# Group norm of the RWKV heads along the free dimension, in an fp32 decoder step on one Trainium2 core

## The chip, the cores and the metric

The kernel runs on one core of one Trainium2 chip. A time is the device time of one execution in microseconds (us); where several executions were timed, the median is given with the lowest and the highest. Names of engines are those of the profile: PE is TensorE's matmul stream and PEld its weight loads, DVE is VectorE, ACT is ScalarE, POOL is GpSimd, SP is SyncE, which here only issues DMAs. PEclk is the TensorE clock that was granted, as a share of full speed.

## The reference, cut to what matters

One trunk layer of a hybrid decoder on 256 prompt tokens and 8 single decode tokens, all in fp32: a half-step SwiGLU, a mixing stage in which attention heads and RWKV-7 heads read one projection and are joined by one output projection, and a second half-step SwiGLU. The change lies in the RWKV heads (16 heads of 64 columns, worked on as 8 pairs):

```python
def wkv_scan(S0, r, logw, k, v, kk, a):
    def step(S, inp):
        r_t, lw_t, k_t, v_t, kk_t, a_t = inp
        sa = jnp.einsum('bhij,bhj->bhi', S, -kk_t)
        S = (S * jnp.exp(lw_t)[:, :, None, :] + sa[..., None] * (kk_t * a_t)[:, :, None, :]
             + v_t[..., None] * k_t[:, :, None, :])
        return S, jnp.einsum('bhij,bhj->bhi', S, r_t)
...
    S, y = wkv_scan(wkv0, r, logw, k, v, kk, a)
    mean = jnp.mean(y, axis=-1, keepdims=True)
    var = jnp.mean((y - mean) ** 2, axis=-1, keepdims=True)
    yn = ((y - mean) * lax.rsqrt(var + GN_EPS)).reshape(B, T, RWKV_WIDTH) * ln_w.astype(f32) + ln_b.astype(f32)
    bonus = jnp.sum(r * k * r_k.astype(f32), axis=-1, keepdims=True) * v
    out = (yn + bonus.reshape(B, T, RWKV_WIDTH)) * g
```

The mean and the variance of the group norm are taken over the 64 columns of one head, for each token apart.

## The kernel before, in words

Every large product is a `gemm` (L141): weights come in chunks of four 128x128 blocks. For a chunk, SP starts a 256 KB load into `raw` (six deep), ACT casts it to `hi` (L137), DVE subtracts to `lo` (L64; four deep), and PE does three matmuls of 128x264 per block into a PSUM tile `acc` (three deep): twice with `hi`, once with `lo`. Line L80 is the helper that issues every matmul, L64 that of two-operand DVE and POOL operations, L67 that of `scalar_tensor_tensor`, L74 that of ACT's functions, so groups in the profile are told apart by the names of their tiles.

The stages follow each other: first SwiGLU, mixing, output projection, second SwiGLU. Mixing (`mixing_body`, L362) runs 38 tiles of the input projection in the order of `SEQ`; after each chunk `tick()` advances every spawned task by one step, and a task is a Python generator that gives up its turn at each `yield`. `pause(n)` gives up n turns. So the constants at the top of the file (`LAG`, `P1`, `P2`, `DWAIT`, `PW`, `HOP`, `NSTEP`) say how many chunks of the gemm lie between two steps of a task. The gemm's matmuls are what stands between the tasks' small products on PE; the order in which the instructions of each engine finally stand is made by the framework's scheduler, and each engine then works its instructions in that order.

The tasks that matter here work on four batches of two head pairs:

- `prep` (L445), one per pair: keys, decays and the tables for the scan; among its small products are `m<-PT,...` to `XD` and `uv`.
- `chain` (L570), one per batch: a triangular inverse on DVE (tiles `X`, `Xt`, `st`; one `yield` per `NSTEP` steps), then 32x32 products (`m<-PT,gm`, `m<-TT,W`), 64x64 products into `ub`, `wb`, `pb`, `gb`, `pN` and `pY`, and a loop over three token blocks in which the state `S` is carried and `pY` is added to. `pY` is the recurrence's output, one 128x512 PSUM tile for a batch. Before, its columns are tokens and its partitions the 64 columns of a head.
- `gnorm` (L727), one per pair, in batches 0, 1 and 2 with `small`: `y` (128x264, the 8 decode columns included) is copied out of `pY` (L694), a product with `cm` from the constants `C` subtracts the mean (`m<-y,C`), ACT squares, three narrow products sum the squares (`m<-C,t`, in `sums`), ACT takes the root, DVE the reciprocal of 88x6, and `spread` (L433) writes that to DRAM (`dr<-s`) and reads it back copied to all 64 partitions of each head (`t<-dr`); then DVE multiplies (`y<-y,t`) and two more DVE operations apply the weights, the bonus and the gate. In batch 3 a product with `bo` sums and spreads the squares in one, and the reciprocal is one of 128x264.
- `turned`, `kvtask`, `attend`, `dec_scores`, `dec_attend`: the attention heads and the decode tokens.

PSUM tiles named `m` form a ring of five banks that all small products share. The output projection takes the eight attention tiles between the pairs 0 to 3 and the pairs 4 to 7 (`PASS`), so batches 2 and 3 are due last.

Of the kernel before, what the change touches and what calls it, by code (L numbers as in the profile page):

```python
# [24 lines left out]
HALF = (slice(0, 64), slice(64, 128))  # L25
# [22 lines left out]
VMU, VKK, VKA, VA0, VRK, VLW, VLB, VSK, VSD = 64, 90, 98, 106, 114, 122, 130, 138, 154  # L48
# [4 lines left out]
def body(tc, I, O):  # L53
    nc = tc.nc
    V, A, G, TE, SP = nc.vector, nc.scalar, nc.gpsimd, nc.tensor, nc.sync
# [3 lines left out]
    def uid(s):  # L59
        cnt[0] += 1  # L60
        return f"{s}{cnt[0]}"

    def tt(e, out, a, b, op):
        return e.tensor_tensor(out=out, in0=a, in1=b, op=op)  # L64

    def stt(out, a, s, b, op0, op1):
        return V.scalar_tensor_tensor(out=out, in0=a, scalar=s, in1=b, op0=op0, op1=op1)  # L67
# [5 lines left out]
    def act(out, in_, f, **k):  # L73
        return A.activation(out=out, in_=in_, func=f, **k)  # L74

    def bc(ap, shape):
        return ap.broadcast_to(list(shape))

    def mm(out, lhsT, rhs, start=True, stop=True, **k):
        return TE.matmul(out, lhsT, rhs, start=start, stop=stop, **k)  # L80
# [20 lines left out]
    def pause(n):  # L101
        for _ in range(n):
            yield

    with ExitStack() as ctx:
# [4 lines left out]
        dp = ctx.enter_context(tc.tile_pool(name="dp", bufs=1, space=bass.MemoryType.DRAM))  # L110
# [16 lines left out]
        def mp():  # L127
            return pp.tile([P, 512], F32, tag="m", bufs=NM, name=uid("m"))
# [33 lines left out]
        eps = cp.tile([P, 2], F32, name="eps")  # L162
# [8 lines left out]
        def vc(i):  # L171
            return vec[:, i:i + 1]
# [189 lines left out]
        def mixing_body(mx, n2, n3, XD, XR):  # L362
# [3 lines left out]
            def ring(shape, tag, bufs):  # L366
                return mx.tile(list(shape), F32, tag=tag, bufs=bufs, name=uid(tag))
# [6 lines left out]
            ident, bo, cm = C[:, CID:CID + P], C[:, CBO:CBO + P], C[:, CCM:CCM + P]  # L374
# [26 lines left out]
            mixed = [None] * 16  # L401
# [21 lines left out]
            la, sgl = fix((P, T), "la"), fix((P, T), "sgl")  # L423
# [1 line left out]
            class Batch:  # L425
                pass

            def sums(sq):
                sm = mp()
                for j in range(3):  # L430
                    mm(sm[0:88, j * 2:j * 2 + 2], sq[:, j:T:3], bo[:, 0:P:64])
                return sm[0:88, 0:6].rearrange("p (j h) -> p h j", h=2)

            def spread(s, to):
                d = dp.tile([2, T], F32, tag=uid("dr"), name=uid("dr"))
                SP.dma_start(d.rearrange("h (p j) -> p h j", j=3), s)
                yield from pause(HOP[0])
                for h in range(2):
                    behind(SP.dma_start(to[HALF[h]], bc(d[h:h + 1], (64, T))))
                yield from pause(HOP[1])  # L440

            def c4(x):
                return x[:, :NP].rearrange("p (c t) -> p c t", c=4)

            def prep(p, bt, k, xrr, xk, xv):  # L445
# [9 lines left out]
                kk, b = tmp(), tmp()  # L455
# [6 lines left out]
                W, Wi = tmp((P, 4, 65)), tmp((P, 4, 64))  # L462
# [40 lines left out]
                tt(V, bv, bps[:, :T], xv, ALU.mult)  # L503
                A.copy(rk[:, T:], bps[:, T:T + 2 * NB])
# [37 lines left out]
                yield  # L542
                gv, dps = mp(), mp()
                for i in range(NB):
                    c, g = i // 2, i % 2
# [24 lines left out]
            def chain(bt):  # L570
# [47 lines left out]
                yield  # L618
                ps = mp()
                for j in range(4 * n):  # L620
                    for h in range(2):
# [5 lines left out]
                yield from pause(P1)  # L627
                Ys = [yb[bt.p0 + k] for k in range(n)]
                uv = bt.UV
                N = ring((P, n, 4, 64), "N", 1)  # L630
                ub, wb = mp(), mp()
# [9 lines left out]
                A.copy(W, v[:, :, 1:4, :])  # L641
# [33 lines left out]
                yield  # L675
                S = N[:, :, 0, :]
                for c in range(1, 4):
                    ps = mp()
                    for k in range(n):
                        x = (k * 4 + c) * 64  # L680
                        for h in range(2):
                            r, o = HALF[h], HALF[1 - h]
                            mm(ps[r, k * 64:k * 64 + 64], PT[r, k, c - 1, :], S[r, k])
                            mm(pY[o, x:x + 64], S[r, k], bt.KR[k][r, 1, c, :], False, True, skip_group_check=True)
                    Z, Sn = ring((P, n, 64), "Z", 2), ring((P, n, 64), "S", 3)
                    for k in range(n):
                        stt(Z[:, k], S[:, k], wc[:, bt.p0 + k, c:c + 1], N[:, k, c, :], ALU.mult, ALU.add)
# [3 lines left out]
                    yield  # L691
                for k in range(n):
                    for h in range(2):
                        (A.copy, V.tensor_copy)[h](Ys[k][HALF[h], :NP], pY[HALF[1 - h], k * NP:(k + 1) * NP])  # L694
# [4 lines left out]
                gps = []  # L699
                gs = [gnorm(Ys[k], SMALL[bt.i]) for k in range(n)]  # L700
                for _ in range(PW[3] + 1 + SMALL[bt.i] * sum(HOP)):
                    for g in gs:
                        next(g)
                    yield
                for k in range(n):
                    p, o = bt.p0 + k, Ys[k]
                    gp = mp()
                    mm(gp[:, :T], g2s[k], sgl)
                    stt(o, o, vc(VLW + p), bt.bv[k], ALU.mult, ALU.add)
                    stt(o, o, vc(VLB + p), gp[:, :T], ALU.add, ALU.mult)  # L710
                    mixed[p] = o
                if len(bts) == nbat and bt is bts[-1]:
                    spawn(turned())
                yield
# [9 lines left out]
                    A.copy(XR[HALF[h], 4], xt[0:64, HALF[h]])  # L724
                yield

            def gnorm(y, small):  # L727
                yp = mp()
                mm(yp[:, :T], cm, y)
                r = tmp()  # L730
                act(r, yp[:, :T], AF.Square)
                if small:
                    A.copy(y, yp[:, :T])
                    yield from pause(PW[3])
                    s = ring((88, 2, 3), "s", 4)
                    act(s, sums(r), AF.Sqrt, scale=1.0 / 64, bias=eps[0:88, 1:2])
                    V.reciprocal(s, s)
                    yield from spread(s, r)
                    tt(V, y, y, r, ALU.mult)
                    yield  # L740
                    return
                yield from pause(PW[3])
                vp = mp()
                mm(vp[:, :T], bo, r)
                act(r, vp[:, :T], AF.Sqrt, scale=1.0 / 64, bias=eps[:, 1:2])
                V.reciprocal(r, r)
                tt(V, y, yp[:, :T], r, ALU.mult)
                yield

            kT, Vt = [None] * 2, [None] * 2  # L750
            dkv = fix((P, 2, 2, NB), "dkv")
# [394 lines left out]
```

## Time and profile before

| | |
|---|---|
| median of 3 executions (lowest, highest) | 1952.91 us (1950.18, 1953.28) |
| profiled execution, its own time | 1950.27 us |
| its span, first to last instruction | 1948.5 us |
| PE busy | 1934.1 us (99%) |
| DVE, ACT, POOL busy | 1307.8, 1035.9, 260.6 us |
| mean granted TensorE clock | 0.997 |

The profile is of one execution. Its waits list how long an engine stood idle and which event ended that; its chain follows the last instruction back, at each step to what released it; its windows give the busy time of every engine in a stretch of the span, with the granted clock. An fp32 matmul leaves more than one record, so a count in the chain (x2) is of records and not of products.

### The profile page before, as it was taken

The page shows a single profiled execution, that of the slowest core. Times are in us where ns is not written, and L with a number is a line of the kernel's source. Part 1 is how long each engine was busy: PE and PEld are TensorE (multiplying, and loading weights), DVE is VectorE, ACT ScalarE, POOL GpSimd, SP SyncE. Part 2 cuts the span into 40 slices and gives each one's busy share as a digit, 9 for nine tenths or more (in the row PEclk, how much of TensorE's full clock was granted, in tenths as well). Part 3 has the DMA queues.
Part 4 walks back from the last instruction along what each step waited for, and adds up shares of the span by engine and source line. Part 5 has one row for each costly group of instructions (what it writes and reads, how often), then busy time and mean ns, then how long its engine had stood idle before and what let it go on. Part 6 is the DMA issues. An engine that isn't in the chain of part 4 may idle for free.

```text
span 1948.5 us, 45522 instructions
## 1 busy us (share of the span) xinstructions
PE 1934.1 (99%) x17131; PEld 1917.4 (98%) x17131; DVE 1307.8 (67%) x2591; ACT 1035.9 (53%) x2069; POOL 260.6 (13%) x382
## 2 busy tenths in 40 slices
PE   9999999999999999999999999999999999999998
PEld 9999999999999999999899999999999999999998
DVE  5865555655556567799867877866666666666665
ACT  5644444444444456666477645644444444444445
POOL 0401102010010112231102100210101001010012
PEclk9999999999999999999999999999999999999999
DMA  7666666665656567565545656566666666666664
GB/s 240 179 194 193 186 194 195 185 189 179 188 182 184 184 193 233 162 173 155 146 133 151 200 157 183 176 187 188 192 191 193 187 193 190 193 194 184 195 181 149
DMA packets 220958, 358.10 MB, mean 184 GB/s; under 512 B 34866, under 2 KB 74434, under 8 KB 220738
## 3 DMA queue, kind: packets, MB, share of 16 engines
q1 hardware_dynamic: 214226, 346.59, 59.6%
q10 hardware_dynamic: 6512, 8.61, 1.3%
q8 instruction: 134, 2.20, 0.4%
q14 instruction: 86, 0.70, 0.1%
HBM read 347.48 MB, written 9.70 MB: 183 GB/s over the span
## 4 chain that ended last, share of the span: by engine, by line
PE 98%; DMA 1%; DVE 1%; ACT 0%; issue 0%; SPq 0%; DVEq 0%; ACTq 0%
PE acc L80 89%; PE m L80 8%; DMA x<-in_x 0%; DMA t<-dr 0%; DVE y L64 0%; DMA ld<-in_cv 0%; PE m L535 0%; DVE lo L64 0%; SPq L581 0%; DMA ld<-in_bias 0%; ACT t L74 0%; PE m L493 0%; PE m L528 0%; PE m L812 0%; ACT hi L137 0%
## 5 line engine op out<-in xcount | busy, mean ns | idle before, releaser
L64 DVE TENSOR_TENSOR lo<-raw,hi 128x512 fp32r<-128x512 f32 (+1 forms) x1288 | 875.6, 683 | 522.8 <-ACT hi L137 499.4
L137 ACT CAST hi<-raw 128x512 fp32r<-128x512 f32 (+1 forms) x1288 | 776.8, 606 | 803.3 <-PE acc L80 724.5
L80 PE MATMUL acc<-x,hi 128*128 128x264 f32 x4840 | 900.2, 287 | 1.5 <-DVE st L64 1.3
L80 PEld LDWEIGHTS acc<-x,hi 128*128 128x128 f32 x4840 | 753.3, 189 | 5.0 <-ACT t L74 1.5
L80 PE MATMUL acc<-x,lo 128*128 128x264 f32 x2420 | 692.8, 286 | 0.0
L80 PE MATMUL acc<-h,hi 128*128 128x264 f32 x2752 | 495.0, 284 | 0.0
L80 PEld LDWEIGHTS acc<-x,lo 128*128 128x128 f32 x2420 | 458.3, 189 | 1.5 <-DVE lo L64 0.4
L80 PEld LDWEIGHTS acc<-h,hi 128*128 128x128 f32 x2752 | 424.4, 189 | 0.0
L80 PE MATMUL acc<-h,lo 128*128 128x264 f32 x1376 | 387.8, 284 | 0.0
L80 PEld LDWEIGHTS acc<-h,lo 128*128 128x128 f32 x1376 | 259.2, 189 | 0.0
L64 POOL TENSOR_TENSOR t<-t,t 128x264 f32<-128x264 f32 x74 | 79.8, 1078 | 1095.6 <-DVE t L64 958.2
L80 PE MATMUL acc<-y,hi 128*128 128x264 f32 x648 | 122.7, 284 | 0.0
L80 PE MATMUL acc<-o,hi 128*128 128x264 f32 x648 | 120.1, 284 | 0.0
L80 PE MATMUL acc<-kv,hi 128*128 128x264 f32 x582 | 109.7, 284 | 0.0
L80 PEld LDWEIGHTS acc<-y,hi 128*128 128x128 f32 x648 | 101.2, 189 | 0.1
L80 PEld LDWEIGHTS acc<-o,hi 128*128 128x128 f32 x648 | 100.1, 189 | 0.0
L67 DVE SCALAR_TENSOR_TENSOR x<-acc,x 128x264 f32<-128x264 f32 x192 | 81.2, 427 | 24.5 <-PE acc L80 23.6
L80 PE MATMUL acc<-y,lo 128*128 128x264 f32 x324 | 92.0, 284 | 0.0
L80 PE MATMUL acc<-o,lo 128*128 128x264 f32 x324 | 92.0, 284 | 0.0
L80 PEld LDWEIGHTS acc<-kv,hi 128*128 128x128 f32 x582 | 90.2, 189 | 0.1
L64 DVE TENSOR_TENSOR t<-acc,t 128x264 f32<-128x264 f32 x156 | 67.4, 432 | 32.8 <-PE acc L80 32.7
L80 PE MATMUL acc<-kv,lo 128*128 128x264 f32 x291 | 82.9, 285 | 0.0
(300 smaller groups left out, 1637.5 us busy)
## 6 DMA issues: line engine op xcount, KB each, us to landing
raw<-in_gu SPq DMA_DIRECT2D x688, 256.0 KB, 3.3
raw<-in_dn SPq DMA_DIRECT2D x224, 256.0 KB, 2.9
raw<-in_win SPq DMA_DIRECT2D x152, 256.0 KB, 3.5
raw<-in_dn SPq DMA_DIRECT2D x160, 192.0 KB, 2.8
raw<-in_wout SPq DMA_DIRECT2D x64, 256.0 KB, 3.5
xsp<-x ACTq DMA_DIRECT2D x16, 132.0 KB, 3.7
x<-xsp SPq DMA_DIRECT2D x16, 132.0 KB, 4.0
ld<-in_sT SPq DMA_DIRECT2D x16, 128.0 KB, 4.4
```

The lines of the kernel that those rows point to most:

```text
L64: return e.tensor_tensor(out=out, in0=a, in1=b, op=op)
L67: return V.scalar_tensor_tensor(out=out, in0=a, scalar=s, in1=b, op0=op0, op1=op1)
L80: return TE.matmul(out, lhsT, rhs, start=start, stop=stop, **k)
L137: A.copy(hi[:, :w], raw[:, :w])
```

## The change

Only the RWKV tasks change.

1. The operands of the products into `pY` are swapped, so that tokens lie on partitions and a head's 64 columns along the free dimension.
2. `gnorm` is now one task per batch, the same for all four: DVE sums `pY` over the free dimension (TENSOR_REDUCE, 128x512 to 128x8), subtracts the mean into the tile `N`, ACT squares, DVE sums the squares, ACT takes the root, DVE the reciprocal (128x24, decode columns included) and multiplies `N`. Sixteen 64x64 products with an identity turn a batch back into a PSUM tile `tp`. The 8 decode columns of each pair still go through `cm` and `bo`, 16 columns for a batch.
3. `sums`, `spread` and their hop through DRAM are gone: six `dr<-s` and twelve `t<-dr` transfers.
4. The copy of `W` moves from ACT to DVE, and the two copies of `uv` swap engines.
5. Pauses: `NSTEP` falls from 5 to 3 (a turn is given up ten times in the inverse, before six times), new pauses `PZ` and `PX` stand where one `yield` stood, and others change their length.

```diff
-LAG = (11, 7, 7, 7)
-P1 = 1
-P2 = 3
-TURN = 2
-SMALL = (1, 1, 1, 0)
-HOP = (2, 2)
-NSTEP = 5
-DWAIT = (11, 10, 11, 3)
-PW = (2, 1, 3, 3, 9)
+LAG = (8, 9, 7, 7)
+P1 = (1, 1, 1, 1)
+P2 = (2, 3, 3, 3)
+TURN = 1
+HOP = 2
+NSTEP = 3
+DWAIT = (11, 12, 11, 3)
+PW = (2, 1, 3, 3, 8)
+PZ = (2, 2, 2, 4)
+PX = (1, 2, 1, 1)
...
-                yield
+                yield from pause(PZ[bt.i])
                 ps = mp()
...
-                A.copy(W, v[:, :, 1:4, :])
+                V.tensor_copy(W, v[:, :, 1:4, :])
                 v = ub[:, :n * 256].rearrange("p (k c t) -> p c k t", k=n, c=4)
                 for h in range(2):
-                    (A.copy, V.tensor_copy)[h](uv[HALF[h], :, :, HALF[h]], v[HALF[1 - h]])
-                yield from pause(P2)
+                    (V.tensor_copy, A.copy)[h](uv[HALF[h], :, :, HALF[h]], v[HALF[1 - h]])
+                yield from pause(P2[bt.i])
...
-                            mm(pY[HALF[1 - h], x:x + 64], uv[:, c, k, HALF[h]], bt.Gm[k][h][:, c, 64:128],
+                            mm(pY[HALF[1 - h], x:x + 64], bt.Gm[k][h][:, c, 64:128], uv[:, c, k, HALF[h]],
...
-                            mm(pY[o, x:x + 64], S[r, k], bt.KR[k][r, 1, c, :], False, True, skip_group_check=True)
+                            mm(pY[o, x:x + 64], bt.KR[k][r, 1, c, :], S[r, k], False, True, skip_group_check=True)
...
-                for k in range(n):
-                    for h in range(2):
-                        (A.copy, V.tensor_copy)[h](Ys[k][HALF[h], :NP], pY[HALF[1 - h], k * NP:(k + 1) * NP])
-                    A.copy(Ys[k][:, NP:T], XD[:, 7, bt.p0 + k, :])
...
+            def gnorm(bt, pY, N, g2s):
...
+                V.tensor_reduce(out=m, in_=y, op=ALU.add, axis=AX.X)
+                stt(yc, bc(m.unsqueeze(2), (P, n4, 64)), -1.0 / 64, y, ALU.mult, ALU.add)
+                dps = mp()
+                mm(dps[:, :nd], cm, yd)
+                sq = ring((P, n * NP + nd), "ysq", 1)
+                act(sq[:, n * NP:], dps[:, :nd], AF.Square)
+                act(sq[:, :n * NP], yc.rearrange("p s t -> p (s t)"), AF.Square)
                 yield from pause(PW[3])
+                mm(dps[:, nd:2 * nd], bo, sq[:, n * NP:])
+                act(r[:, n4:], dps[:, nd:2 * nd], AF.Sqrt, scale=1.0 / 64, bias=eps[:, 1:2])
+                V.tensor_reduce(out=m, in_=sq[:, :n * NP].rearrange("p (s t) -> p s t", t=64), op=ALU.add, axis=AX.X)
+                act(m, m, AF.Sqrt, scale=1.0 / 64, bias=eps[:, 1:2])
                 V.reciprocal(r, r)
+                tt(V, yc, yc, bc(m.unsqueeze(2), (P, n4, 64)), ALU.mult)
+                tt(V, sq[:, :nd], dps[:, :nd], r[:, n4:], ALU.mult)
+                yield from pause(HOP)
+                tp = mp()
+                for k in range(n):
+                    for c in range(4):
+                        x = (k * 4 + c) * 64
+                        for h in range(2):
+                            o = HALF[1 - h]
+                            mm(tp[HALF[h], x:x + 64], yc[o, k * 4 + c, :], ident[o, o])
+                for k in range(n):
+                    p, o = bt.p0 + k, yb[bt.p0 + k]
+                    gp = mp()
+                    mm(gp[:, :T], g2s[k], sgl)
+                    stt(o[:, :NP], tp[:, k * NP:(k + 1) * NP], vc(VLW + p), bt.bv[k][:, :NP], ALU.mult, ALU.add)
+                    stt(o[:, NP:], sq[:, k * NB:(k + 1) * NB], vc(VLW + p), bt.bv[k][:, NP:], ALU.mult, ALU.add)
+                    stt(o, o, vc(VLB + p), gp[:, :T], ALU.add, ALU.mult)
+                    mixed[p] = o
```

What stands in a row on the engines, at three places (a name is the written tile, then what it is read from; numbers behind a name count the tiles; x16 is sixteen in a row).

First, PE at the end of batch 1's run of small products, before: `XD`, `uv` are the last of `prep`'s products, `TT,W` the inverse's last 32x32 ones, `acc` the gemm.

```order
L80 MATMUL m_13455<-XD,ld_13330 64x2
L80 MATMUL m_13454<-uv_11879,gm_13282 64x64
L80 MATMUL m_13455<-XD,ld_13330 64x2 x3
L80 MATMUL m_13454<-uv_11879,gm_13324 64x64
L80 MATMUL m_13506<-TT_12420,W_13137 32x32 x16
L80 MATMUL acc_13831<-x_106,hi_13833 128x264
L80 MATMUL acc_13831<-x_106,lo_13834 128x264
```

Ahead of these rows stand, with no gemm matmul between, 16 `PT,gm`, the other `XD,ld` (32 in all) and the other `uv,gm` (16 in all), so 80 small products stand in a row. The same engine at the same place of the changed kernel, where `TT,W` now stands:

```order
L81 MATMUL acc_13643<-x_109,lo_13774 128x264
L81 MATMUL acc_13825<-x_106,hi_13827 128x264 x2
L81 MATMUL acc_13825<-x_106,lo_13828 128x264
L81 MATMUL m_13753<-TT_12453,W_13392 32x32 x16
L81 MATMUL acc_13825<-x_106,hi_13827 128x264 x2
L81 MATMUL acc_13825<-x_106,lo_13828 128x264
```

The 80 have moved apart: 61 in a row (ten that `prep` issues ahead, the `XD,ld` and `uv,gm`, three of the attention), then 28 gemm matmuls, then 16 `PT,gm` with four products of the attention, 15 gemm matmuls, and the 16 `TT,W`.

Second, DVE at batch 0's group norm, before: `y<-y,t` wait for the transfer `t<-dr`, and `lo`, `st`, `Xt` and the projection's `t<-acc,rs` stand between and behind them.

```order
L64 TENSOR_TENSOR t_13485<-acc_13237,rs 128x264
L64 TENSOR_TENSOR y_112<-y_112,t_12989 128x264
L64 TENSOR_TENSOR lo_13618<-raw_13616,hi_13617 128x512
L64 TENSOR_TENSOR st_13030<-X_12413,Xt_12414 128x60
L64 TENSOR_TENSOR lo_13639<-raw_13637,hi_13638 128x512
L67 SCALAR_TENSOR_TENSOR y_112<-y_112,vec,t_10936 128x264
L64 TENSOR_TENSOR y_112<-y_112,t_12994 128x264
```

After, at the same group norm; `yr` holds the sums and then the reciprocals, `N` the centred values, `ysq` the squares.

```order
L704 TENSOR_REDUCE yr_13001<-m_12794 128x8
L448 RECIPROCAL t_12879<-m_12966 128x264
L65 TENSOR_TENSOR Xt_12447<-Xt_12447,st_13142 128x5x13
L68 SCALAR_TENSOR_TENSOR N_12693<-yr_13001,m_12794 128x512
L65 TENSOR_TENSOR lo_13403<-raw_13401,hi_13402 128x512
L65 TENSOR_TENSOR lo_13487<-raw_13485,hi_13486 128x512
L68 SCALAR_TENSOR_TENSOR t_12879<-t_12879,t_12878 128x264
L65 TENSOR_TENSOR st_13163<-X_12446,Xt_12447 128x60
L65 TENSOR_TENSOR lo_13522<-raw_13520,hi_13521 128x512
L714 TENSOR_REDUCE yr_13001<-ysq_13006 128x8
```

No DVE instruction of the group norm waits for a DMA any more; the second TENSOR_REDUCE waits for ACT's squares, with the inverse and the weights' `lo` queued behind it.

Third, PE at batch 0's group norm, before: one `cm` product (`m<-y,C`) and three narrow sums (`m<-C,t`), between gemm matmuls.

```order
L80 MATMUL m_12992<-y_112,C 128x264
L80 MATMUL acc_13099<-x_108,lo_13191 128x264
L80 MATMUL m_13045<-t_12954,C 128x264
L80 MATMUL acc_13099<-x_108,hi_13190 128x264 x2
...
L80 MATMUL acc_13099<-x_109,hi_13212 128x264
L80 MATMUL m_13119<-C,t_12989 88x2 x3
```

After, the identity products of the same batch (`m<-C,N`), with the gate's two products (`sgl,ld`) that stood there before too:

```order
L81 MATMUL acc_13558<-x_108,hi_13607 128x264 x2
L81 MATMUL m_13172<-t_13018,C 128x280
L81 MATMUL m_13199<-C,N_12693 64x64 x16
L81 MATMUL m_13216<-sgl,ld_12997 128x264
L81 MATMUL m_13221<-sgl,ld_12999 128x264
L81 MATMUL m_13235<-kr_12535,bk_12534 128x128 x4
L81 MATMUL acc_13558<-x_108,lo_13608 128x264
```

Two `cm` products and six sums of a batch have given way to sixteen 64x64 products, which wait for the last DVE operation on `N`, and to two of 128x16 for the decode columns.

More of the change, by code (lines that the diff above doesn't have):

```diff
@@ L426, in mixing_body @@
                 pass
[L428 to L437, printed above, removed]
-                for h in range(2):
-                    behind(SP.dma_start(to[HALF[h]], bc(d[h:h + 1], (64, T))))
-                yield from pause(HOP[1])
             def c4(x):
@@ L505, in prep @@
                 bt.near += 1
-                yield
+                yield from pause(PX[0])
                 while bt.near < bt.n:
@@ L541, in prep @@
                 bt.BT[k] = BT
-                yield
+                yield from pause(PX[1])
                 gv, dps = mp(), mp()
@@ L617, in chain @@
                     A.copy(zs[r], ps[r, :n * P].rearrange("p (c t) -> p c t", t=32))
-                yield
+                yield from pause(PZ[bt.i])
                 ps = mp()
@@ L626, in chain @@
                     A.copy(TT[r, :, 32:64], ps[r, :n * P].rearrange("p (c t) -> p c t", t=32))
-                yield from pause(P1)
-                Ys = [yb[bt.p0 + k] for k in range(n)]
+                yield from pause(P1[bt.i])
                 uv = bt.UV
@@ L674, in chain @@
                    bc(wc[:, bt.p0:bt.p0 + n, :].unsqueeze(3), (P, n, 4, 64)), ALU.mult)
-                yield
+                yield from pause(PX[3])
                 S = N[:, :, 0, :]
@@ L690, in chain @@
                     S = Sn
-                    yield
-                for k in range(n):
-                    for h in range(2):
-                        (A.copy, V.tensor_copy)[h](Ys[k][HALF[h], :NP], pY[HALF[1 - h], k * NP:(k + 1) * NP])
-                    A.copy(Ys[k][:, NP:T], XD[:, 7, bt.p0 + k, :])
+                    yield from pause(PX[2])
                 for k in range(n):
@@ L698, in chain @@
                 g2s = [load(I["g2"][bt.p0 + k], (P, P)) for k in range(n)]
[L699 to L711, printed above, removed]
+                yield from gnorm(bt, pY, N, g2s)
                 if len(bts) == nbat and bt is bts[-1]:
@@ L725, in turned @@
                 yield
[L727 to L741, printed above, removed]
+            def gnorm(bt, pY, N, g2s):
+                n = bt.n
+                n4, nd = 4 * n, n * NB
+                y, yc = (x.rearrange("p (s t) -> p s t", t=64) for x in (pY[:, :n * NP], N.rearrange("p k c t -> p (k c t)")))
+                yd = XD[:, 7, bt.p0:bt.p0 + n, :].rearrange("p k b -> p (k b)")
+                r = ring((P, n4 + nd), "yr", 1)
+                m = r[:, :n4]
+                V.tensor_reduce(out=m, in_=y, op=ALU.add, axis=AX.X)
[5 more added lines that the diff above has]
+                act(sq[:, :n * NP], yc.rearrange("p s t -> p (s t)"), AF.Square)
@@ L742, in gnorm @@
                 yield from pause(PW[3])
-                vp = mp()
-                mm(vp[:, :T], bo, r)
-                act(r, vp[:, :T], AF.Sqrt, scale=1.0 / 64, bias=eps[:, 1:2])
+                mm(dps[:, nd:2 * nd], bo, sq[:, n * NP:])
+                act(r[:, n4:], dps[:, nd:2 * nd], AF.Sqrt, scale=1.0 / 64, bias=eps[:, 1:2])
+                V.tensor_reduce(out=m, in_=sq[:, :n * NP].rearrange("p (s t) -> p s t", t=64), op=ALU.add, axis=AX.X)
+                act(m, m, AF.Sqrt, scale=1.0 / 64, bias=eps[:, 1:2])
```

2 lines of the change are left out of this document (removed).

## The prediction

> **What bounds the kernel now.** I read the page first, to see which engine is full.
>
> ```profile
> span 1948.5 us, 45522 instructions
> PE 1934.1 (99%) x17131; PEld 1917.4 (98%) x17131; DVE 1307.8 (67%) x2591; ACT 1035.9 (53%) x2069; POOL 260.6 (13%) x382
> ```
>
> PE is busy for 1934.1 of 1948.5 us. So a change can gain in two ways only: less work on PE, or fewer of the 14.4 us in which it stands still. DVE's 67% is a mean over stages. Next, what PE waited for in the middle of the span (the four longest):
>
> ```profile
> PE m L80 <- issue: 1.7, 1, 1.7
> PE acc L80 <- DVE st L64: 1.3, 1, 1.3
> PE m L80 <- ACT t L504: 1.1, 1, 1.1
> PE m L80 <- POOL eps L164: 1.0, 1, 1.0
> ```
>
> The columns are total, times, longest. The 1.0 belongs to the start, the 1.3 to the attention's bias load, by the chain of waits (start, length, what):
>
> ```profile
> 1068.81 2.11 DMA ld<-in_bias
> ...
> 1075.90 1.11 PE acc L80 x7
> ```
>
> The change touches neither. The other two lie inside the RWKV tasks. The chain tells what is behind the 1.1:
>
> ```profile
> 905.99 0.45 PE m L80 x2
> ...
> 910.14 0.61 PE m L80 x6
> ...
> 920.30 0.43 DVE t L64
> ...
> 921.12 3.90 DMA t<-dr
> ...
> 925.12 0.12 DVE y L64
> ...
> 925.69 0.60 DVE lo L64
> 926.29 0.35 DVE t L64
> ...
> 926.66 0.18 ACT t L504
> ...
> 926.89 0.71 PE m L80 x2
> ```
>
> PE's late product needed ACT's `t`, which needed DVE's `t`, which stood behind DVE's `y<-y,t`, and that waited for batch 0's statistics to come back from DRAM: 3.90 us of transfer. The wait list's name (ACT) is the last link only. The first rows also give prices: one `cm` product is two records, 0.45 us; three `sums` products are six, 0.61 us, so 0.20 each. Now the 1.7 us, in batch 1's inverse:
>
> ```profile
> 937.75 3.09 PE m L80 x120
> 940.84 1.66 issue
> 942.50 0.43 PE m L80 x7
> 942.93 4.92 PE acc L80 x21
> 947.85 1.61 PE m L80 x54
> ...
> 953.03 2.87 PE m L80 x112
> ...
> 957.45 0.39 PE m L80 x16
> ...
> 958.26 2.55 PE acc L80 x21
> ```
>
> A run of 120 records without a gemm matmul, 1.66 us in which PE waited for nothing that the profile shows, and then 21 gemm matmuls in 4.92 us, for which 21 others took 2.55 (0.12 each). The windows name the reason:
>
> ```profile
> core 0: us, PE busy (x) PEld busy (x) DVE busy (x) ACT busy (x) POOL busy (x), PEclk, DMA share, GB/s
> 940.00:942.00 2.00, 0.84 (x42) 0.73 (x38) 0.33 (x2) 0.54 (x3) 0.82 (x5) 1.00 0.98 301
> 942.00:943.00 1.00, 0.50 (x9) 0.43 (x8) 0.00 (x0) 0.04 (x1) 0.00 (x0) 0.57 0.98 221
> 944.00:946.00 2.00, 2.00 (x11) 2.00 (x11) 0.69 (x1) 0.62 (x1) 0.00 (x0) 0.50 0.76 252
> 949.00:950.00 1.00, 1.00 (x33) 0.93 (x27) 0.00 (x0) 0.48 (x1) 0.31 (x1) 1.00 0.62 139
> ```
>
> The granted clock is 0.50 behind the pause and back at 1.00 from 949 on. Half the clock cost 4.92 − 2.55 = 2.37 us on the gemm, 1.61 − 54 × 0.0245 = 0.29 on the 54 records (0.39/16 = 0.0245 each at full clock), and 0.43 − 7 × 0.0245 = 0.26 on the seven: 2.9 us. Six microseconds at half speed bound it at 3.1; the gemm rows alone give 2.4.
>
> **The change part by part.** *PE's work.* Batches 0 to 2 lose two `cm` products and six sums each: 2 × 0.45 + 2 × 0.61 = 2.12, three times 6.4 us. Batch 3 loses two `cm` and two `bo` products of the same shape: 1.8. Together 8.2. Each batch gains sixteen 64x64 identity products; eight such products of the scan are the sixteen records of the row at 957.45, so 16 × 0.049 = 0.78 (0.051 by the row at 953.03). And it gains two of 16 columns, which the trace doesn't have: between a tiny product (0.05) and one of 264 columns (0.45), nearest the sums' 0.20 since the weights are as wide; so 0.40 (0.1 to 0.9). Four batches: 4.7 (3.5 to 6.9). All of it is on the path, since PE is full. Net **−3.5** (−4.7 to −1.3).
>
> *The DRAM hop.* With `spread` no DVE instruction of the group norm waits for a DMA, and SP's queue is rid of 18 entries between weight loads. The 1.06 us before 926.89 go (wait list: 1.1). What is late next there is the same product's own DVE operations, 0.3 us ahead of it by the chain (926.29, 926.66), which then run 3 us earlier. **−1.1** (−1.1 to 0).
>
> *The dense run.* In the order of the program, 80 small products stand there in a row; after, there are 61 (13 of them larger ones), then 28 gemm matmuls, 16 and 4, 15 gemm matmuls, and 16. I read the pause as PE running out of instructions:
>
> ```profile
> q8 instruction: 134, 2.20, 0.4%
> ```
>
> The program comes in 134 pieces of 16 KB (2.20 MB/134), and a run of 120 records in 3.09 us uses them some five times as fast as the gemm (0.026 us a record against 0.12), just when the DMA engines are 98% busy. The run of 112 records at 953.03 had no pause behind it, so the edge lies about there. The 48 tiny products left in a row are under the 56 of that run, and 28 gemm matmuls (3.4 us) follow. So pause and half clock go: **−1.7 and −2.9** (0 to −4.8). This is the largest and the least sure term.
>
> [...]
>
> *DVE's work.* Rows of DVE in the mixing stage (count | busy, mean ns | idle before), and one of ACT:
>
> ```profile
> L67 DVE SCALAR_TENSOR_TENSOR y<-y,vec,t 128x264 f32<-128x264 f32 x8 | 3.9, 482 | 0.0
> L746 DVE RECIPROCAL t<-t 128x264 f32<-128x264 f32 x2 | 3.6, 1798 | 1.4 <-ACT t L74 1.4
> L694 DVE COPY y<-m 64x256 f32<-64x256 f32 x8 | 3.3, 418 | 0.9 <-ACT y L694 0.7
> L64 DVE TENSOR_TENSOR N<-m,wc 128x512 f32<-128x512 f32 x4 | 2.8, 690 | 1.3 <-PE m L80 1.3
> L64 DVE TENSOR_TENSOR y<-y,t 128x264 f32<-128x264 f32 x6 | 2.6, 432 | 3.2 <-DMA t<-dr 3.1
> L737 DVE RECIPROCAL s<-s 88x6 f32<-88x6 f32 x6 | 0.9, 166 | 1.2 <-ACT s L74 1.2
> ```
>
> ```profile
> L641 ACT COPY W<-m 128x384 f32<-128x384 f32 x4 | 1.9, 481 | 0.1
> ```
>
> A batch of 0 to 2 loses two of each but `N`, L746: 2 × (0.482 + 0.418 + 0.432 + 0.166) = 3.0 us. It gains the copy of `W` (0.5), the subtraction and the multiplication on 128x512 (2 × 0.69), two TENSOR_REDUCE of 128x512, the reciprocal of 128x24 (0.3, between 0.166 for 6 columns and 1.8 for 264), and for the pairs 2 × 0.48 and three of 8 or 16 columns (0.17 as L737). TENSOR_REDUCE is not in the trace: between the 0.42 of a copy and 512 columns at the reciprocal's rate, 512/264 × 1.8 = 3.5. I take 0.69, by the one row with as many elements. That makes 5.0 us, **+2.0** a batch (1.5 to 7.6). Batch 3 loses 2 × 1.8 in exchange: −1.2. Whether PE feels it is told by the stretches in which the batches end:
>
> ```profile
> 890.00:920.00 30.00, 30.00 (x362) 28.75 (x361) 28.32 (x90) 18.39 (x42) 4.67 (x14) 1.00 0.46 126
> 950.00:1000.00 50.00, 50.00 (x565) 47.84 (x565) 42.64 (x171) 36.13 (x103) 4.52 (x12) 1.00 0.50 139
> ```
>
> Batch 0 has 1.7 us free and needs 2.0: 0.3 short. From 950 on there are 7.4 us free, which cover 2.0. I take **+0.7**, twice the shortage, since batch 1's inverse and its group norm now stand closer to each other; nothing (four chunks of `lo` lie ahead) to 6.0 (no cover in three batches at 2.0, or batch 0 alone at 7.6, 7.6 − 1.7 = 5.9; the others have 7.4 free).
>
> *The new waits and moved steps.* In each batch DVE's second TENSOR_REDUCE waits for ACT's square of 128x512, and the reciprocal for a root; queued behind are `lo` and the inverse's `st`, for which PE waits. Three turns of the gemm lie between square and sum: 3 × 12 × 0.12 = 4.3 us against some 1.2 for two such DVE and ACT operations, so I add nothing. The identity products wait for `N`; two turns (2.9 us) cover 0.69. `W` on DVE needs about as long as on ACT, and 2.9 us or more of gemm (`P2`, two turns) hide it. The longer pauses delay the batches, but the last one is due only at the third part of the output projection: 136 gemm matmuls, 16.3 us, are left between its last product and the first that reads it. ACT, 36.13 of 50 us busy, takes 512 columns of squares and gives away the copies. All nothing.
>
> **Sum**, against the profiled execution's own 1950.27: −3.5 − 1.1 − 1.7 − 2.9 + 0.7 = −8.5, so 1941.8. The median of the runs shown, 1952.91, lies 2.6 above that execution; with half of it added, since either may be the usual one, **1943.1 us**.
>
> **The rivals.**
> - *The pause stays* (1.7 and 2.9 come back): it is due to the moment, with DMA at 98%, or another dense run meets it: 16 identity, two gate and four key products now stand in a row. For it: the row says "issue", which names no cause. Against it: one such pause in 1948 us, behind the longest run. 1943.1 + 4.6 = 1947.7. [...]
> - *Only the half clock stays*, by a cause apart from the pause (the activity of tiny products, say): 1943.1 + 2.9 = 1946.0. [...] Against it: the clock was 1.00 until the pause.
> - *DVE gives the gain back*: DVE's operations find no cover (6.0 in place of 0.7) and the 16-column products cost 0.45 (2.2 more): 1943.1 + 5.3 + 2.2 = 1950.6, no change. For it: 28.32 of 30.
> - *Slower: the square on ACT blocks DVE.* DVE works in order; if the sum of squares comes to its front before ACT has squared, `lo` is late, PE stands still as long as here (1.66) and loses the clock (2.9): 4.6 a batch. All four: 1943.1 + 18.4 = 1961.5; it is slower from three batches on (1956.9 against the bound 1956.8). For it: the chain above is such a blockade, and there are two new waits a batch. Against it: that one had a transfer of 3.90 us, this one 4.3 us of cover.
>
> **How the numbers follow.** Forecast 0.54, pause stays 0.12, half clock stays 0.06, DVE 0.15, slower 0.13. About 0.2% (3.9 us) is what a measurement of this kernel can tell from no change; faster is below 1949.0. The forecast and the first two rivals lie below, less the 0.04 of them that spread over it: faster 0.68; same 0.15 + 0.04 = 0.19; slower 0.13. The low end takes the best bounds, 1950.27 − 4.7 − 1.1 − 4.8 = 1939.7, less 1.7 for an unforeseen second of the small waits: 1938. The high end takes the third rival with the full 2.6 of the runs: 1950.6 + 1.3 = 1952, and 1 us more for a part of the fourth: 1953.
>
> **What would show it.** PE's count is free of `m<-C,t`, its busy time is 3 to 4 us less than 1934.1 beyond the half-clock part; no `t<-dr` in the chain; no "issue" row over 1 us and clock 1.00 in every window of the mixing stage; DVE's TENSOR_REDUCE rows near 690 ns. A PE wait on `N`, on `lo` behind `yr`, or a clock of 0.50 anywhere between the first product of batch 0 and the output projection would make it wrong.

## The result, and the profile after

Over 14 executions of each kernel the change makes no difference: 1952.69 us (1950.82 to 1955.51) against 1952.81 us, ratio 1.0002 with a 95% interval of 0.9994 to 1.0010. The forecast was 1943.1 us. The profiled execution took 1952.84 us. Each ratio in this text is the recorded estimate over all executions, and can differ from the quotient of the two medians by some 0.0003.

The page of the changed kernel, its first lines:

```profile
span 1951.0 us, 45640 instructions
## 1 busy us (share of the span) xinstructions
PE 1935.2 (99%) x17219; PEld 1917.4 (98%) x17219; DVE 1310.5 (67%) x2603; ACT 1028.2 (53%) x2043; POOL 258.4 (13%) x382
```

PE is no less busy than before (1934.1), though by the forecast it has less to do. What PE waited for (total, times, longest):

```profile
PE m L81 <- DMA ld<-in_kc: 3.1, 1, 3.1
...
PE m L81 <- DVE Xt L65: 0.9, 1, 0.9
PE m L81 <- ACT kr L538: 0.7, 2, 0.6
...
PE m L81 <- ACT kr L518: 0.5, 1, 0.5
PE m L748 <- issue: 0.2, 1, 0.2
```

The pause named "issue" (1.7) and the wait on batch 0's statistics (1.1, `ACT t`) are gone, as forecast. In their place stands the longest wait of all, 3.1 us for `ld<-in_kc`, in a part of the kernel that the forecast never looked at: the decode tokens' scores, which need a key cache in four pieces of 128 KB. The chain of waits there, in order of time:

```profile
1070.16 4.64 DMA raw<-in_wout
...
1074.86 3.73 DMA raw<-in_wout
...
1078.61 0.39 SPq L932
...
1079.04 4.28 DMA ld<-in_kc
...
1083.36 1.02 PE m L81 x4
```

SP's queue was at work on other things until 1079.0, and only then issued the load. What it did, from SP's timeline (start, length, line, transfer), first of the changed kernel:

```profile
1067.10 0.33 SPq L372 DMA_DIRECT2D ld<-in_kc  x1
...
1068.12 1.94 SPq L932 DMA_DIRECT2D x<-xsp  x3
...
1070.58 3.28 SPq L932 DMA_DIRECT2D x<-xsp  x7
...
1077.14 1.85 SPq L932 DMA_DIRECT2D x<-xsp  x4
1079.04 0.43 SPq L372 DMA_DIRECT2D ld<-in_kc  x1
```

and of the kernel before:

```profile
1072.30 1.15 SPq L371 DMA_DIRECT2D ld<-in_kc  x2
1073.54 2.60 SPq L946 DMA_DIRECT2D x<-xsp  x5
```

Before, the fourth key load stood ahead of the sixteen reloads of the residual (`x<-xsp`, 132 KB each, for the output projection); after, it stands behind them. No line of the change names either transfer. The scheduler orders SP's queue anew for the changed program; which part of the change moves the load isn't isolated. Windows of the changed kernel (start and end, then length and busy time of PE, PEld, DVE, ACT and POOL, each with its number of instructions; then clock, DMA share, GB/s) show what the wait cost beyond itself:

```profile
1076.00:1080.00 4.00, 4.00 (x36) 4.00 (x35) 3.83 (x21) 3.46 (x14) 0.00 (x0) 1.00 0.88 254
1080.00:1082.00 2.00, 0.26 (x3) 0.04 (x1) 2.00 (x8) 1.15 (x3) 0.00 (x0) 1.00 0.96 304
1084.00:1088.00 4.00, 4.00 (x15) 3.64 (x16) 0.00 (x0) 0.21 (x1) 0.00 (x0) 0.50 0.72 230
1098.00:1102.00 4.00, 4.00 (x35) 3.90 (x33) 3.57 (x14) 1.76 (x4) 0.72 (x1) 1.00 0.51 143
1103.00:1106.00 3.00, 3.00 (x16) 3.00 (x15) 1.87 (x10) 1.28 (x3) 0.00 (x0) 0.50 0.32 97
```

The clock falls to 0.50 at the end of the wait, and again at 1103, with no idle PE ahead of it. By the clock's own records the two stretches last 6.83 and 3.41 us, and the first begins at 1082.4, 1.0 us before the wait ends. If PE's matmuls follow the clock there, half of the other 9.3 us, so 4.6, is lost, and with the wait 7.7: nearly the forecast's 8.5.

### The profile page after: what moved, and what is told of

It reads as the page before. It is cut to its first block, busy times and chain, and to the rows that moved or that the text cites. A ratio compares the mean times of both kernels' runs of the same rounds, so it can differ in the third digit from the quotient of the medians.

```text
span 1951.0 us, 45640 instructions
## 1 busy us (share of the span) xinstructions
PE 1935.2 (99%) x17219; PEld 1917.4 (98%) x17219; DVE 1310.5 (67%) x2603; ACT 1028.2 (53%) x2043; POOL 258.4 (13%) x382
## 4 chain that ended last, share of the span: by engine, by line
PE 96%; DVE 1%; ACT 1%; DMA 1%; issue 0%; POOL 0%; DVEq 0%; SPq 0%; ACTq 0%; POOLq 0%
PE acc L81 88%; PE m L81 7%; DMA raw<-in_wout 0%; DVE lo L65 0%; ACT t L75 0%; DMA ld<-in_kc 0%; ACT hi L138 0%; DVE y L65 0%; DVE t L791 0%; ACT kr L518 0%; PE m L522 0%; DVE st L65 0%; DVE Xt L65 0%; ACT BT L527 0%; DMA raw<-in_win 0%
```

## The experiments

Theory: the gains of the forecast came, and one late load gave them back. Rivals: the gains never came (the pause was a matter of the moment), or the load is only one of several things late there.

**Both kernels a second time.** Before:

> The kernel before, unchanged, profiled a second time. Theory (the stalls come from the order in which instructions stand, so they come back in every execution): PE's pause of about 1.7 us named issue behind the 80 small products of batch 1, about 6.8 us of half clock behind it, and the 1.1 us wait in batch 0's group norm, are all there again; span within 2 us of 1948.5. Rival (the pause was a matter of the moment, with the DMA engines full): no such pause, no half clock in the mixing stage, span about 1944.

After:

> The changed kernel, unchanged, profiled a second time. Theory (the fourth load of the key cache stands on SP's queue behind sixteen reloads of the residual x, so it is late in every execution): PE waits 2.5 to 3.7 us for that load again, with half clock behind it, and shows no pause named issue over 1 us. Rival (a slow transfer in one execution): the wait is under 1 us and the span about 1944.

Spans 1950.7 and 1953.7 us, the first 2.2 above its forerunner and so just outside what was expected. Every stall came back at its place. From PE's waits, before and after:

```profile
PE m L80 <- issue: 2.6, 1, 2.6
PE m L80 <- ACT t L504: 1.4, 1, 1.4
```

```profile
PE m L81 <- DMA ld<-in_kc: 3.3, 1, 3.3
```

Half clock followed each as in the first profiles: 6.83 us before; 6.83 and 6.83 us after. Neither is a matter of the moment.

**The key load alone put right.**

```diff
-                    kc = load(I["kc"][p, b // 2], (P, 2, P))
+                    with tc.high_priority():
+                        kc = load(I["kc"][p, b // 2], (P, 2, P))
```

> The changed kernel, with the four loads of the key cache of each half of the heads at the scheduler's high priority; on SP the fourth moves from behind the sixteen reloads of x to behind the first of them, and nothing else moves by more than a few places. Theory (the forecast gains came, and the late key load gave them back): the wait of 3.1 us and the half clock behind it, 6.8 and 3.4 us long, go; that is 3.1 + some 4.5 us, so 0.9961 of the kernel before (0.9950 to 0.9975), about 1945 us, no half clock before the tail. Rival (the wait only names the last of several things that were late at that place, softmax of the last heads or the weights of the output projection): PE stands still there nearly as long for another cause, ratio 0.999 to 1.001.

Measured: 1945.91 us (8 executions) against 1952.09, **ratio 0.9971 (0.9961 to 0.9981)**. The page's first and third line, and PE's waits:

```profile
span 1943.8 us, 45643 instructions
...
PE 1929.7 (99%) x17219; PEld 1912.4 (98%) x17219; DVE 1310.7 (67%) x2603; ACT 1028.0 (53%) x2043; POOL 259.7 (13%) x382
```

```profile
PE m L81 <- DVE Xt L65: 1.1, 1, 1.1
PE acc L81 <- ACT hi L138: 1.0, 1, 1.0
...
PE m L81 <- ACT kr L538: 0.8, 2, 0.6
...
PE m L81 <- ACT kr L518: 0.5, 1, 0.5
```

No wait for the load, and no half clock before the kernel's tail. SP now issued the fourth key load at 1069.8 in place of 1079.0:

```profile
1069.78 0.38 SPq L372 DMA_DIRECT2D ld<-in_kc  x1
```

PE's order in the two traces is the same but for four records of that load's own products and a few of the gemm's beside them. So putting that load right gave some 6 us (1.0002 − 0.9971 = 0.0031 of 1952), and the change without the late load is worth 5.7 us (0.0029 × 1952). The theory holds. A second profile:

> The changed kernel with the key loads moved, profiled a second time. Theory: no wait for the key load, no pause named issue over 0.5 us, span 1943 to 1945 without half clock before the tail; 1.7 to 3.5 us more if the decode attention falls into half clock. Rival (the first profile was a lucky execution): a wait of over 1.5 us that the first didn't show.

Span 1944.8 us, the same waits (`Xt` 1.1, `hi` 1.1, `kr` 0.8 and 0.5), no half clock.

**The reloads taken off SP instead.**

```diff
-                SP.dma_start(xr[o], xsp[o])
+                A.dma_start(xr[o], xsp[o])
```

> The changed kernel, with the sixteen reloads of x issued by ACT's queue in place of SP's, so that SP's key loads and the output projection's weights stand behind none of them. Theory (SP's queue made the fourth key load late): no wait for the key load, ratio 0.997 (0.996 to 0.998) as for a_kchi, unless ACT, which now issues sixteen transfers in order, makes hi late. Rival (the reloads compete for the DMA engines, whichever queue issues them): a wait of over 1.5 us for the key load or a weight load in that stretch, ratio 0.999 or more.

1949.18 us (1946.63 to 1951.16), ratio 0.9982 (0.9973 to 0.9991), just outside what was expected, and no wait for a key load: SP's order was the cause, and not that the reloads fill the DMA engines. It gives back 3.9 us (0.0020 × 1952) and not 6, with executions 4.5 us apart; unlike the edit above it also moves dozens of PE's matmuls in this stretch. A second profile:

> The changed kernel with the reloads of x on ACT's queue, profiled a second time; its eleven executions lay between 1946.6 and 1951.2 and the profiled one, without half clock before the tail, was 1946.8. Theory (the spread comes from half clock in the decode attention, which falls into one execution and not into another): an execution of 1949 us or more shows 3.4 or 6.8 us of half clock between 1095 and 1112 us, one below 1947.5 shows none. Rival (the spread has another source): the time is above 1949 with clock 1.00 all through, or below 1947.5 with half clock.

This execution took 1950.43 us, and it had 6.83 us of half clock from 1100.3 on. PE was never idle ahead of it:

```profile
1090.00:1100.00 10.00, 10.00 (x84) 9.90 (x84) 9.67 (x41) 5.29 (x15) 0.73 (x1) 1.00 0.61 191
1100.00:1104.00 4.00, 4.00 (x22) 4.00 (x21) 2.87 (x17) 0.77 (x3) 0.00 (x0) 0.53 0.49 147
```

Half of 6.83 is 3.4, and PE's busy time is 2.8 us longer (1933.7 against 1930.9), of the 3.7 us between the two profiled executions (1950.43 and 1946.77). The eleven executions say the same: the two whose mean granted clock was 0.998 took 1946.6 and 1946.8, the nine at 0.996 or 0.997 took 1948.4 to 1951.2. The spread of this kernel is in good part whether this stretch falls into half clock. It also means that the 6 us above hold a part of this kind: the load put right left this stretch at full clock in both of its profiles, and the reloads on ACT did so in one of two.

**What makes the pause?** The forecast said: the 80 small products in a row. First, the 80 made fewer in the kernel before.

```diff
-LAG = (11, 7, 7, 7)
+LAG = (11, 9, 7, 7)
```

(with the key loads at high priority, as above; in the kernels further down that name it, too)

> The kernel before with LAG of batch 1 at 9 in place of 7, which takes the sixteen TT,W products out of the run of 80 small products (the longest run of small products is then 71, thirteen fewer of them tiny and five of 128x128, and TT,W stand apart), and with the key loads at high priority so that none stands behind the reloads of x. Theory (the run of 80 empties PE's instruction supply, the pause brings the half clock): no pause over 1 us, no half clock in the mixing stage, ratio 0.9976 (0.9965 to 0.9990). Rival (the pause is not due to the run's length): pause and half clock are still there or come elsewhere, ratio 0.9995 to 1.001.

1953.34 us, ratio 1.0009 (1.0000 to 1.0018). The pause and its half clock are gone, but other waits came or grew:

```profile
PE acc L80 <- DVE lo L64: 2.1, 1, 2.1
PE m L80 <- ACT t L504: 1.4, 1, 1.4
PE m L80 <- DVE o L67: 1.3, 1, 1.3
```

The 2.1 is again `lo` behind `y<-y,t`, which waits for the hop through DRAM, and 3.41 us of half clock begin with it. So this doesn't isolate the pause. Next, more in a row, 135 (`LAG` of batch 1 at 5, key loads at high priority):

> The kernel before with LAG of batch 1 at 5 in place of 7 and the key loads at high priority: the longest run of small products grows from 80 to 135 (28 kr,TT, 32 XD,ld, 16 uv,gm, 56 products with W and uv, 3 of the attention). Theory (PE uses its instructions faster than they are brought in such a run, so a pause comes once the supply is empty and a longer run meets it at least once): one or two pauses named issue in or behind the run, 1.7 us or more together, and half clock behind. Rival (the pause at the 80 has nothing to do with the length): no such pause near this run.

1972.53 us, a single execution, **and no pause named issue at all**, against what I expected. But PE waits for other engines in and behind that run (`DVE N` 4.1, `ACT W` 1.5), so its products don't come close together and this run can't decide. The next can, where the 80 stand in a row unchanged:

```diff
-LAG = (8, 9, 7, 7)
-P2 = (2, 3, 3, 3)
-TURN = 1
-NSTEP = 3
-DWAIT = (11, 12, 11, 3)
-PW = (2, 1, 3, 3, 8)
-PZ = (2, 2, 2, 4)
-PX = (1, 2, 1, 1)
+LAG = (11, 7, 7, 7)
+P2 = (3, 3, 3, 3)
+TURN = 2
+NSTEP = 5
+DWAIT = (11, 10, 11, 3)
+PW = (2, 1, 3, 3, 9)
+PZ = (1, 1, 1, 1)
+PX = (1, 1, 1, 1)
```

> The changed kernel with the pauses of before (LAG, P2, TURN, NSTEP, DWAIT, PW as before, PZ and PX at 1) and the key loads at high priority: the new group norm, the swapped operands and the moved copies alone. The run of 80 small products in a row stands there again. Theory (group norm and hop give 4.6 us, the dense run's pause is due to the pauses between steps): PE shows the pause named issue of 1.7 to 2.6 us with 6.8 us of half clock, no wait at batch 0's statistics; without another new wait 0.998 (0.997 to 0.999); the key loads stand behind the sixteen reloads here, so a wait for them of up to 3.3 us with half clock may come on top, 1.001. Rival (the pause is not made by the run's length): no pause named issue, clock 1.00 there.

1956.55 us, ratio 1.0019 (1.0011 to 1.0028). It is slower for other waits: 3.1 us for `DVE W`, the copy that the change moved to DVE, 2.8 for `ACT BT` and 1.4 for `DVE st`, with 3.41 us of half clock behind the second; there was none for a key load. The chain at the 80 products:

```profile
939.61 3.21 PE m L81 x128
942.83 1.05 PE acc L81 x7
```

3.2 us and no pause: the theory as I had put it falls. (The chain's rows leave records out; the trace has all 160 of the 80 products there, 0.020 us each, and in the kernel before 152 ahead of the pause.) The trace's DMA records offer another. Queue q8, `instruction` on the page, brought 134 packets of 16 KB while PE worked off 17131 matmul records and as many weight loads, on average a packet for every 128 records, so 256 instructions each. Up to 750 us they begin 112 to 144 records apart, so I take them for PE's. In the kernel before one such packet runs from 939.89 to 941.08; this is the view of the transfers from 939.8 to 941.2:

```profile
q8 instruction: 1, 0.02, 5.3%
```

PE stops at 940.84 and goes on at 942.50. In the second profile the packet runs from 941.49 to 942.37, PE stops at 941.26 and goes on at 943.91. Both times PE goes on 1.4 to 1.5 us after the packet has landed, and both times in the middle of the sixteen `TT,W`, behind the 24th of their 32 records. If a block begins at the record behind it and every 128 records from there, each packet up to 750 us in the first profile begins 106 to 126 records ahead of its block, nearly one whole block, and the one at 939.89 only 37 ahead; that is an estimate, since no record says what a packet holds. In the kernel above the packet comes at 943.30, when the gemm is running again. So it seems that not the length decides, but where the edge of a block lies in the run. That can be tested by moving the edge alone:

```diff
-NWARM = 11
+NWARM = 10
...
         for _ in range(NWARM):
             mm(warm[:, :P], ones, ones)
+        for _ in range(33):
+            mm(warm[0:32, 0:32], ones[0:32, 0:32], ones[0:32, 0:32])
```

> The kernel before, with one of its eleven warming products at the start replaced by 33 of 32x32. All engines keep their order behind that, the run of 80 small products too; only PE's stream is 64 matmul records longer ahead of it, half of a block of 256 instructions (a matmul record and its weight load are two). Theory (PE's instructions come in 16 KB blocks, one ahead; a dense run starves PE only if a whole block lies within it, so the place of the block's edge decides): the edge moves 64 records forward in the run, no block lies within it, no pause named issue over 0.5 us and no half clock behind it; 1.7 to 2.6 + 2.9 us less, ratio 0.9976 (0.9965 to 0.9988). Rival (the pause belongs to this instruction or to the DMA load at that moment): pause of 1.7 us or more at the same product, ratio 0.9995 to 1.0005.

The same place, the same 80 products:

```profile
938.82 3.21 PE m L80 x128
942.03 2.74 PE acc L80 x21
```

No pause, and the 21 gemm matmuls take 2.74 us where they took 4.92 and 4.61. The packet comes at 942.90, behind the run. With the stream 64 records longer ahead of it, the same run passes without the pause, as the theory said. The time hardly follows: 1951.46 us, ratio 0.9993 (0.9984 to 1.0002), where 0.9965 to 0.9988 was expected. The profiled execution, the longest with 1955.40 us, had 10.24 us of half clock in the decode attention from 1100.2 on. Its wait at batch 0's statistics grew to 1.8 us, and waits of 0.8 and 0.5 us for ACT are new. Six of the eleven executions had a mean granted clock of 0.998, as the profile of the changed kernel with the load put right, and still took 1949.6 to 1952.5. Why the 4.6 us of the pause don't come off in full isn't settled.

**The pauses alone** (the kernel before with all new pauses, old group norm, key loads at high priority):

> The kernel before with the new pauses alone (LAG, P2, TURN, NSTEP, DWAIT, PW, PZ, PX) and the key loads at high priority: the old group norm with its hop through DRAM. No run of small products is longer than 59. Theory: no pause named issue over 1 us and no half clock behind it, 4.6 to 5.5 us less; the statistics come back from DRAM as late as before, so some wait on them stays, and the narrow sums and cm products stay on PE; ratio 0.9975 (0.996 to 0.9995), as long as no other wait of over 1.6 us brings the half clock. Rival (the new pauses fit only the new group norm): new waits of 2 us and more on DVE and a half clock at one of them, ratio 1.000 to 1.003.

1966.29 us, **ratio 1.0070 (1.0056 to 1.0083)**: the rival's way, and worse. No pause named issue over 0.2 us; but the chain runs through the hop, and three half-clock stretches of 3.41 us stand between 937 and 975 (a fourth at 1115):

```profile
925.95 3.98 DMA dr<-s
...
930.57 4.29 DMA t<-dr
...
934.95 0.43 DVE y L66
935.38 0.60 DVE gm L66
```

The new pauses bring batch 1's work onto DVE while batch 0's `y<-y,t` still waits for DRAM. Neither half of the change pays without the other: the new pauses come to 1.0070 with the old group norm, the new group norm to 1.0019 with the old pauses, both together to 0.9971, each with the key loads put right.

**The identity products twice** (with the key loads put right):

```diff
-                            mm(tp[HALF[h], x:x + 64], yc[o, k * 4 + c, :], ident[o, o])
+                            for _ in range(2):
+                                mm(tp[HALF[h], x:x + 64], yc[o, k * 4 + c, :], ident[o, o])
```

> The changed kernel with the key loads moved (as a_kchi), and each of the 64 identity products of 64x64 issued twice to the same place. Theory (PE is full, so every added product is paid, 0.049 us each): 64 x 0.049 = 3.1 us over a_kchi, about 1949.0, ratio 0.9987 (0.998 to 0.9995). Rival (PE waits at those places for DVE anyway, so that the doubled products are hidden): within 1 us of a_kchi, ratio 0.997.

1952.99 us, ratio 1.0001 (0.9993 to 1.0010) against 0.9971 with one each, so they are paid, and more than in full. In the profiles PE's busy time rises by 7.7 us (1937.4 against 1929.7), of which 3.4 are half of a half-clock stretch of 6.83 us from 1101.5 on; 4.3 are left, 0.067 for each product, not 0.049. The timeline of the single ones, one batch:

```profile
927.51 1.15 PE L81 MATMUL m<-C,N 64*64 64x64 f32 x32
928.59 1.16 PE L81 MATMUL m<-sgl,ld 128*128 128x264 f32 x4
```

Sixteen products (32 records) in the 1.08 us from start to start: 0.067 each again.

## Why the prediction was wrong, point by point

- **The sum left out a queue.** The step that failed is the last of the change part by part: of the moved steps only the batches' due time was weighed ("136 gemm matmuls, 16.3 us"), and SP's queue only as rid of 18 entries. That the last key load and the reloads of `x` had changed places on it stood in the order of the program, and the margin before was short: PE's products with the last key pieces ran at 1083, the reloads were issued until 1086. What the runs showed in its place is a wait of 3.1 us for that load and half clock behind it; the price was some 6 us when the load alone was moved, 3.9 when the reloads were. The same paragraph put every other new wait at nothing; they came to 3.4 us, below.
- *DRAM hop, −1.1:* right in place and size (the wait is gone; it was 1.1 and 1.4).
- *Dense run, −1.7 and −2.9:* the pause and the half clock went, and the runs speak for the supply of instructions as the cause (64 records more ahead of the run took the pause away); the criterion (a run of more than some 112 records) was wrong. It was also read from rows of the chain, which leave records out: 152 stood ahead of the pause, not 120. Runs of 80 products pass without a pause in two kernels. So the length alone, 80 there too, didn't make the pause; what the shift changed is where in the run the next 128 records begin. That the changed kernel is free of it comes from its run being shorter or its edges lying elsewhere; which, isn't settled.
- *PE's work, −3.5:* too large. PE's busy time fell from 1934.1 to 1929.7 with the load put right; less the forecast's 2.9 of half clock that is −1.5. The identity products cost 0.067 and not 0.049, 4.3 in place of 3.1 us; the other 0.8 isn't located.
- *DVE, +0.7:* the durations were right, below, but the waits too small. The stretches from which the cover was read (890 to 920, 950 to 1000) hold the group norms of batches 0 and 1 alone; those of batches 2 and 3 begin at 1024 and 1134. With the load put right `Xt` 1.1, `hi` 1.0, `kr` 0.8 and 0.5 are new, 3.4 us, while the attention's 1.3 (`DVE st`), which the forecast left standing, is gone: net 2.1.

```profile
L704 DVE TENSOR_REDUCE yr<-m 128x8 f32<-128x512 f32 x4 | 2.7, 680 | 0.0
L714 DVE TENSOR_REDUCE yr<-ysq 128x8 f32<-128x512 f32 x4 | 2.7, 680 | 0.1
L627 DVE COPY W<-m 128x384 f32<-128x384 f32 x4 | 2.2, 556 | 0.1
L716 DVE RECIPROCAL yr<-yr 128x24 f32<-128x24 f32 x4 | 1.2, 301 | 2.8 <-ACT yr L75 2.8
```

- *The sum with these in it*, against the first profiled execution: −1.5 − 1.7 − 2.9 − 1.1 + 2.1 = −5.1, measured 1943.8 − 1948.5 = −4.7 in the span. The forecast's −8.5 was 3.4 too much even without the key load.
- *The rivals:* none of the four was it. The third named this outcome, no change, but by 6.0 us of DVE's waits, where all new waits came to 2.1 net; that its result came out is chance. The square on ACT never blocked DVE for as long as 1.66 us; the half clock that stayed in the total came from a new place.

## What to carry to other kernels

When a change moves steps that feed a scheduler, compare the order of every queue over the whole stage, not only around the edit: the price here lay some 160 us behind the first group norm that was changed, in two transfers that no line of the diff names. Where PE is full, a wait cost nearly twice its length here: behind the 3.1 us the clock stood at 0.50 for 6.83 us, PE was at work for 5.9 of them, and half of that, 2.9, is lost by the estimate above. It need not: in the changed kernel with the old pauses PE stood still for 3.15 us from 950.35 on, and the clock stayed at 1.00 (the next gemm matmuls began 0.12 us apart, from 956.59 on). And when an expected gain doesn't show, look for the new longest wait first: the edit that removed it, one line around one load statement, gave the best version here (0.9971).

## What the runs showed of the hardware

- **The half clock lasted 3.41, 6.83 or 10.24 us at a time.** So it was with each stretch in the middle of these kernels. They followed waits of 1.66, 2.6, 3.1 and 3.3 us, but not the 3.15 and 1.83 us that PE stood still in two other kernels, and came also without any idle PE, in the decode attention: 27 of the 80 matmul records that begin between 1095 and 1106 in the changed kernel's first profile stream eight columns against 128x128 weights. In the first profiles of the two kernels, little was streamed in the 3.41 us ahead of such a fall: columns times the used part of the array came to 0.06 of full before the one at 942.15 (kernel before), and to 0.32 and 0.22 before those at 1082.39 and 1102.87 (after; the gemm, 264 columns on the whole array every 0.12 us, taken as full). In steps of 3.41 us from these falls, five more stretches between 10 and 1935 us were as poor, 0.27 to 0.40, at full clock and without a fall behind them, so this is a correlation and no rule.
- **Twice, by these records, a packet of instructions came late.** In the kernel before the packets begin once in 128 matmul records on average, and 130 of the 134 landed within 0.88 to 1.5 us (median 0.97, longest 2.28); after the two pauses PE went on only 1.4 and 1.5 us behind the landing, and 128 records of small products are gone in as little as 2.6 us, at 0.020 us each. The pauses were 1.66 and 2.64 us. They fell into runs worked at 0.021 us a record (152 records in the 3.16 us to 940.84, first profile); at the gemm's pace, 0.12 us a record, none came: that profile's list of PE's waits has only the 1.66 under issue.
